# A two-layer encoder trunk: Hyena's transforms modulo 4, their first half moved into the attention, the filter's last layer in high and low parts

## The chip, the cores and the metric

The kernel runs on one core of a Trainium2 chip. The metric is the device time of one execution in microseconds (us), a median over several executions. One further execution is recorded by the hardware profiler. Engines are PE (matrix products; PEld is its loading of stationary operands), DVE and ACT (elementwise work), POOL and SP (here almost only issuers of transfers).

## The reference, cut to what matters

Layer 1 of the trunk has two mixers side by side, a dense attention of eight heads and a Hyena convolution over 512 channels, then a projection with `w_out`. What the change touches is Hyena: a filter made by a small sine network, and a long convolution by Fourier transforms.

```python
def hyena_filter(L, w1, b1, w2, b2, w3, b3, w4, freq):
    ...
    h = (h @ w4.astype(f32)).reshape(L, 2, CONV_WIDTH)
    deltas = jnp.abs(jnp.linspace(HYENA_MIN_DECAY, HYENA_MAX_DECAY, CONV_WIDTH, dtype=f32))
    h = h * jnp.exp(-t[:, :, None] * deltas)
    kfull = jnp.concatenate([h[:, 0], jnp.zeros((1, CONV_WIDTH), f32), h[:0:-1, 1]], axis=0)
    return kfull * lax.rsqrt(jnp.sum(kfull * kfull, axis=0, keepdims=True) + EPS)

def fft_long_conv(u, kfull):
    L = u.shape[1]
    uf = jnp.fft.rfft(u.astype(jnp.float32), n=2 * L, axis=1)
    kf = jnp.fft.rfft(kfull, n=2 * L, axis=0)
    return jnp.fft.irfft(uf * kf[None], n=2 * L, axis=1)[:, :L].astype(u.dtype)

def mixer_cd(...):
    q, k, v = split_qkv(h, qk_g)
    att = blocked_dense_attention(axial_rope(q), axial_rope(k), v)
    u = short_conv(h[..., QKV_COLS:], conv_w, conv_b)
    x0, x1, vh = jnp.split(u, 3, axis=-1)
    kfull = hyena_filter(h.shape[1], f_w1, f_b1, f_w2, f_b2, f_w3, f_b3, f_w4, f_freq)
    z = x1 * vh
    y = x0 * (fft_long_conv(z, kfull) + skip * z)
    return jnp.concatenate([att, y], axis=-1)
```

The sequence is 512 tokens long, the model 1024 wide, everything float32.

## The kernel before, in words

**Layout.** Activations stand channels by tokens, eight tiles of 128 channels by 512 tokens. A dense product in full precision is made of three products of rounded parts: an operand is split into a high part (ACT casts it, line L203) and a low part (DVE subtracts, L204), and PE adds high x high, low x high and high x low. Weights arrive as 128x1024 tiles `raw`, are split into `wh` and `wl`, and are used in `column` (L224 to L226) and `project` (L358, with the residual update on DVE at L363). Small products that are not split are plain float32 matmuls; in the trace each of those is two records.

**Order.** Every engine works through its own queue in order. A scheduler fixes that order when the program is built; pools of tiles add waits. A pool has a fixed number of slots, and a tile that takes a slot waits until the last reader of the slot's former tile is done. The pools that matter here are `x` (8 slots of 128x512), `e3` (2), `wh` and `wl` (5 each), and the banks of the accumulators: A has 3, V 1, Q 2, C 2.

**The filter.** `hyena_filter` (L1011) runs while layer 0's last feed-forward projection is on PE. The last layer multiplies the 64-row `fsrc` by `w4` in 8 plain float32 matmuls of 512 columns (L1029); DVE multiplies by the decay (L1035), sums squares (L1041, L1042), forms sums and differences (L1045) and splits them. Then 96 matmuls of 256 columns (`dft_sums`, through L224 to L226) transform the filter for two halves of the channels and two parts `ft` of the frequencies, `fold` (L970) combines even and odd tokens, and the spectra go to a scratch tensor `spec` (L1073).

**The attention and Hyena.** In `mixer` of layer 1 a loop over j (pairs of heads) issues a query pair, the softmax of heads 2j and 2j+1 (scores L809 and L810 into bank A, row maxima L820 on DVE, exponentials L825 on ACT into `x` tiles, normalisation L834), the attention of the head before (transposes L847, splits into `e3` tiles, products L853 and L854), and `hyena_in(j)`, which needs three dense columns of 24 matmuls each in bank C. After the loop `hyena` runs for both halves: transposes of z (L1093), per half and `ft` a forward transform of 8 float32 matmuls of 256 columns (L1114), a copy on ACT (L974), the fold (L975, L976), products with the filter's spectrum on DVE (L1123, L1124, L1129) whose spectrum tiles arrive through `x` slots (L1105 to L1107), and per tile j an inverse transform of 8 float32 matmuls (L1140), closed by L1144, L1147 and L1150. The projection with `w_out` (`project`, L358) takes the attention's tiles first, so that its matmuls for those stand between Hyena's on PE.

Of the kernel before, what the change touches and what calls it, by code (L numbers as in the profile page):

```python
# [16 lines left out]
F32 = mybir.dt.float32  # L17
# [7 lines left out]
P = 128  # L25
# [99 lines left out]
def constants():  # L125
# [7 lines left out]
    c[:, 132:136] = -t.reshape(2, P, 2).transpose(1, 2, 0).reshape(P, 4)  # L133
# [23 lines left out]
    m = np.arange(256, dtype=np.int64)  # L157
    mats = []
    for fn in (np.cos, np.sin):
        for par in (0, 1):  # L160
            ph = np.outer(2 * m + par, 2 * m + 1) % 2048
            mats.append(fn(ph * (math.pi / 1024)).astype(f))

    def rows(m):
        return m.reshape(2, P, 256).transpose(1, 0, 2).reshape(P, 512)

    dft = np.ascontiguousarray(np.stack(
        [np.concatenate([rows(mats[q]), rows(mats[q + 1])], axis=1) for q in (0, 2)]
        + [np.concatenate([rows(mats[q].T), rows(mats[q + 1].T)], axis=1) for q in (0, 2)]
    ))  # L170
# [17 lines left out]
class Trunk:  # L188
# [26 lines left out]
    def dft_matrix(self, u):  # L215
        hi, lo = self.t("wh", (P, 1024), F32R), self.t("wl", (P, 1024), F32R)
# [676 lines left out]
    def mixer(self, l, key):  # L893
# [22 lines left out]
        for j in range(4):  # L916
# [41 lines left out]
    def dft_sums(self, mats, sp_cos, sp_sin, tags):  # L958

        out = []  # L960
        for par in range(2):
            p = self.ps(tags[par])
            for q, sp in enumerate((sp_cos, sp_sin)):
                for mt in range(2):
                    lhs = [m[:, par * 512 + mt * 256 + self.ft * P :][:, :P] for m in mats[q]]
                    self.mm3(p[:, q * 256 : q * 256 + 256], lhs, sp[par][mt], mt == 0, mt == 1)
            out.append(p)
        return out

    def fold(self, pe, po, plus, minus):  # L970

        nc = self.nc
        o = self.t("th")
        nc.scalar.copy(out=o, in_=po)  # L974
        nc.vector.tensor_add(out=plus, in0=pe, in1=o)  # L975
        nc.vector.tensor_sub(out=minus, in0=pe, in1=o)  # L976
# [34 lines left out]
    def hyena_filter(self):  # L1011

        nc, ap = self.nc, self.ap
        src = self.fsrc
        w4 = self.t("raw", (P, 1024))[:64]
        nc.sync.dma_start(out=w4, in_=ap["f_w4"])
        delta = self.t("rb")
        nc.sync.dma_start(out=delta, in_=ap["delta"])
        asp, bsp = [[], []], [[], []]
# [229 lines left out]
```

## Time and profile before

| | us |
|---|---|
| median of 3 executions | 1874.56 (1872.99 to 1875.28) |
| profiled execution, its time | 1871.36 |
| its span, first to last instruction | 1869.6 |
| PE busy | 1827.3 (98% of the span) |
| DVE busy | 1527.1 (82%) |
| ACT busy | 980.6 (52%) |

The profiled execution is 3.2 us under the median. Its mean granted PE clock is 0.995 of full speed. A busy share is the share of the span in which the engine had an instruction in work; PE's records overlap, so the distance between the starts of two records tells the price of one.

### The profile page before, as it was taken

The page shows a single profiled execution, that of the slowest core. Times are in us where ns is not written, and L with a number is a line of the kernel's source. Part 1 is how long each engine was busy: PE and PEld are TensorE (multiplying, and loading weights), DVE is VectorE, ACT ScalarE, POOL GpSimd, SP SyncE. Part 2 cuts the span into 40 slices and gives each one's busy share as a digit, 9 for nine tenths or more (in the row PEclk, how much of TensorE's full clock was granted, in tenths as well). Part 3 has the DMA queues.
Part 4 walks back from the last instruction along what each step waited for, and adds up shares of the span by engine and source line. Part 5 has one row for each costly group of instructions (what it writes and reads, how often), then busy time and mean ns, then how long its engine had stood idle before and what let it go on. Part 6 is the DMA issues. An engine that isn't in the chain of part 4 may idle for free.

```text
span 1869.6 us, 29686 instructions
## 1 busy us (share of the span) xinstructions
PE 1827.3 (98%) x11628; PEld 1630.7 (87%) x11628; DVE 1527.1 (82%) x2604; ACT 980.6 (52%) x1610; POOL 3.6 (0%) x9
## 2 busy tenths in 40 slices
PE   7999989999999999999999999999999999999999
PEld 5789879888888899799988988979887898898997
DVE  8998879688759889898799996977887879695682
ACT  5435335378837445255563544655788365353460
POOL 0000000000000000000000000000000000000000
PEclk9999989999999999999999999999999999999999
DMA  7863754733232645745326462345222322233231
GB/s 273 280 218 124 263 179 146 237 110 96 91 99 69 201 145 161 275 147 199 127 72 213 163 215 71 103 163 176 80 80 91 125 90 91 91 113 113 91 125 57
DMA packets 83654, 269.22 MB, mean 144 GB/s; under 512 B 10024, under 2 KB 13352, under 8 KB 83514
## 3 DMA queue, kind: packets, MB, share of 16 engines
q1 hardware_dynamic: 81898, 263.13, 42.2%
q0 software_dynamic: 1616, 4.20, 0.6%
q8 instruction: 91, 1.49, 0.3%
q14 instruction: 49, 0.40, 0.1%
HBM read 258.88 MB, written 10.50 MB: 144 GB/s over the span
## 4 chain that ended last, share of the span: by engine, by line
PE 72%; DVE 15%; DMA 9%; ACT 2%; issue 2%; SPq 0%; ACTq 0%; DVEq 0%
PE pA L486 23%; PE pC L358 16%; DVE wl L204 4%; PE pA L358 4%; PE pV L486 4%; DMA raw<-w_mod 3%; DVE raw L248 3%; PE pC L225 2%; PE pC L226 2%; PE pC L224 2%; PE pA L226 2%; DMA raw<-w2b 2%; PE pA L225 2%; PE pA L224 2%; DMA raw<-w 2%
## 5 line engine op out<-in xcount | busy, mean ns | idle before, releaser
L203 ACT CAST wh<-raw 128x1024 fp32r<-128x1024 f32 (+2 forms) x387 | 368.8, 956 | 453.5 <-PE pA L486 134.4
L204 DVE TENSOR_TENSOR wl<-raw,wh 128x1024 fp32r<-128x1024 f32 (+2 forms) x387 | 426.8, 1105 | 78.7 <-ACT wh L203 74.7
L486 PE MATMUL pA<-h,wh 128*128 128x256 f32 x1608 | 297.2, 283 | 8.5 <-DVE tq L518 7.4
L486 PE MATMUL pA<-e,wh 128*128 128x256 f32 x1608 | 295.5, 281 | 5.7 <-ACT tq L517 4.8
L486 PEld LDWEIGHTS pA<-h,wh 128*128 128x128 f32 x1608 | 247.5, 190 | 12.3 <-DVE tq L518 7.8
L486 PEld LDWEIGHTS pA<-e,wh 128*128 128x128 f32 x1608 | 245.8, 189 | 10.8 <-ACT tq L517 8.6
L486 PE MATMUL pA<-h,wl 128*128 128x256 f32 x804 | 226.6, 282 | 0.2 <-DVE wl L204 0.2
L358 PE MATMUL pC<-gb,wh 128*128 128x512 f32 (+1 forms) x800 | 224.8, 367 | 0.0
L486 PE MATMUL pA<-e,wl 128*128 128x256 f32 x804 | 224.4, 279 | 0.0
L248 DVE SCALAR_TENSOR_TENSOR raw<-raw,cond 128x1024 f32<-128x1024 f32 x144 | 175.1, 1220 | 31.1 <-DMA raw<-w_mod 29.7
L358 PE MATMUL pC<-ga,wh 128*128 128x512 f32 (+1 forms) x648 | 186.2, 372 | 7.1 <-DVE x L363 6.6
L358 PEld LDWEIGHTS pC<-gb,wh 128*128 128x128 f32 x800 | 143.6, 188 | 26.9 <-issue 0.8
L486 PEld LDWEIGHTS pA<-h,wl 128*128 128x128 f32 x804 | 151.5, 188 | 0.5 <-DVE wl L204 0.4
L486 PEld LDWEIGHTS pA<-e,wl 128*128 128x128 f32 x804 | 151.3, 188 | 0.0
L358 PEld LDWEIGHTS pC<-ga,wh 128*128 128x128 f32 x648 | 115.2, 189 | 33.6 <-DVE x L363 12.3
L358 PE MATMUL pC<-gb,wl 128*128 128x512 f32 (+1 forms) x392 | 143.4, 366 | 0.0
L363 DVE SCALAR_TENSOR_TENSOR x<-pC,mod,x 128x512 f32<-128x512 f32 (+1 forms) x108 | 73.2, 685 | 83.1 <-PE pC L358 82.6
L226 PE MATMUL pA<-h,wl 128*128 128x256 f32 (+1 forms) x373 | 118.7, 324 | 3.9 <-DVE wl L204 3.9
L225 PE MATMUL pA<-h,wh 128*128 128x256 f32 (+1 forms) x373 | 119.3, 327 | 1.3 <-DVE h L345 1.3
L224 PE MATMUL pA<-h,wh 128*128 128x256 f32 (+1 forms) x373 | 116.0, 323 | 0.0
L358 PE MATMUL pC<-ga,wl 128*128 128x512 f32 (+1 forms) x300 | 110.4, 368 | 0.0
L486 PE MATMUL pV<-h,wh 128*128 128x256 f32 x536 | 99.4, 284 | 0.5 <-DVE tc L557 0.5
(316 smaller groups left out, 3589.2 us busy)
## 6 DMA issues: line engine op xcount, KB each, us to landing
raw<-w SPq DMA_DIRECT2D x164, 512.0 KB, 3.7
raw<-w_mod SPq DMA_DIRECT2D x144, 512.0 KB, 4.2
raw<-w2b SPq DMA_DIRECT2D x64, 512.0 KB, 4.1
raw<-w_in SPq DMA_DIRECT2D x36, 512.0 KB, 4.3
raw<-w2a SPq DMA_DIRECT2D x32, 384.0 KB, 3.7
raw<-w_out SPq DMA_DIRECT2D x16, 512.0 KB, 3.5
raw<-w_start SPq DMA_DIRECT2D x8, 512.0 KB, 5.0
xs<-x SPq DMA_DIRECT2D x16, 256.0 KB, 2.2
```

The source lines that it names most:

```text
L203: self.nc.scalar.copy(out=hi, in_=src)
L204: self.nc.vector.tensor_sub(out=lo, in0=src, in1=hi.bitcast(F32))
L224: mm(out, lhsT=wh, rhs=rh, start=start, stop=False)
L225: mm(out, lhsT=wh, rhs=rl, start=False, stop=False)
L226: mm(out, lhsT=wl, rhs=rh, start=False, stop=stop)
L248: nc.vector.scalar_tensor_tensor(out=raw, in0=raw, scalar=1.0, in1=self.cond, op0=ALU.mult, op1=ALU.mult, accum_out=m[:, c : c + 1])
L358: nc.tensor.matmul(ps, lhsT=lh, rhs=r, start=k == 0 and q == 0, stop=k == n_in - 1 and q == len(todo) - 1)
L363: nc.vector.scalar_tensor_tensor(out=x, in0=ps, scalar=gate[dt], in1=x, op0=ALU.mult, op1=ALU.add)
L486: self.nc.tensor.matmul(out, lhsT=lh, rhs=rr, start=first and n == 0, stop=n == 11, skip_group_check=True)
```

## The change

The transforms split tokens modulo 4 instead of into even and odd ones. Each of the four matrices is 128x512 instead of two tiles of that size; the forward transform of a half is 8 float32 matmuls of 256 columns instead of 16, the inverse transform of a tile j is 8 float32 matmuls of 128 columns instead of 8 of 256, and the filter's transform is 72 split matmuls instead of 96. More is left to DVE: the fold has two stages, and a butterfly stands behind the products. `hyena` takes one half per call. Half 0 is called behind `hyena_in(2)`, inside the attention loop, half 1 where both were called before. Its `h` tiles for half 0 become `gb` tiles, and its matrices live in `gc` and `rb` slots. The filter's last layer multiplies high and low parts: `w4` is loaded twice, into partitions 0 to 63 and 64 to 127, cast and split, and each of the 8 plain matmuls becomes two rounded ones.

```diff
@@ mixer
                 zs.append(self.hyena_in(j, oth[j]))
+                if j == 2:
+                    self.hyena(0, zs, oth, "gb")
...
-        ys = oth if l == 0 else self.hyena(zs, oth)
-        for j, y in enumerate(ys):
+        if l == 1:
+            self.hyena(1, zs, oth, "h")
+        for j, y in enumerate(oth):
             ready(4 + j, y, "h")
@@ fold
+    def fold(self, p, k, swapped=None):
+        nc = self.nc
+        c, d = self.t("tc"), self.t("tc")
+        nc.scalar.copy(out=c, in_=p[2])
+        nc.scalar.copy(out=d, in_=p[3])
+        e, o = self.t("tq"), self.t("tq")
+        nc.vector.tensor_add(out=e, in0=p[0], in1=c)
+        nc.vector.tensor_add(out=o, in0=p[1], in1=d)
+        nc.vector.tensor_add(out=k[0][0], in0=e, in1=o)
+        nc.vector.tensor_sub(out=k[0][1], in0=e, in1=o)
+        e, o = self.t("tq"), self.t("tq")
+        a, b = slice(0, 256), slice(256, 512)
+        nc.vector.tensor_sub(out=e[:, a], in0=p[0][:, a], in1=c[:, a])
+        nc.vector.tensor_sub(out=e[:, b], in0=c[:, b], in1=p[0][:, b])
+        if swapped:
+            p1, p3 = swapped()
+            d = self.t("tc")
+            nc.scalar.copy(out=d, in_=p3)
+            nc.vector.tensor_sub(out=o, in0=p1, in1=d)
+        else:
+            nc.vector.tensor_sub(out=o[:, a], in0=p[1][:, b], in1=d[:, b])
+            nc.vector.tensor_sub(out=o[:, b], in0=p[1][:, a], in1=d[:, a])
+        nc.vector.tensor_add(out=k[1][0], in0=e, in1=o)
+        nc.vector.tensor_sub(out=k[1][1], in0=e, in1=o)
@@ hyena_filter
+        w4 = self.t("raw", (P, 1024))
+        for half in (slice(0, 64), slice(64, 128)):
+            nc.sync.dma_start(out=w4[half], in_=ap["f_w4"])
+        w4h, w4l = self.t("wh", (P, 1024), F32R), self.t("wl", (P, 1024), F32R)
+        nc.scalar.copy(out=w4h, in_=w4)
+        nc.vector.tensor_sub(out=w4l[:64], in0=w4[:64], in1=w4h[:64].bitcast(F32))
+        src = self.t("tc", dtype=F32R)
+        nc.scalar.copy(out=src[:64], in_=self.fsrc)
+        nc.vector.tensor_sub(out=src[64:], in0=self.fsrc, in1=src[:64].bitcast(F32))
...
-                nc.tensor.matmul(p, lhsT=toks, rhs=w4[:, s * T : (s + 1) * T], start=True, stop=True)
+                nc.tensor.matmul(p, lhsT=toks, rhs=w4h[:, s * T : (s + 1) * T], start=True, stop=False)
+                nc.tensor.matmul(p, lhsT=toks[:64], rhs=w4l[:64, s * T : (s + 1) * T], start=False, stop=True)
...
+            p = [self.dft_sums(mats, asum, bsum, s, "QAQA"[s]) for s in range(4)]
+            k = [[self.t("th"), self.t("th")] for _ in range(2)]
+            self.fold(p, k, lambda: [self.dft_sums(mats, asum, bsum, s, t, True) for s, t in ((1, "A"), (3, "V"))])
@@ hyena
+        p = [self.ps(bank) for bank in "CQCQ"]
+        for s in (0, 2, 1, 3):
+            for q in range(2):
+                nc.tensor.matmul(
+                    p[s][:, q * 256 : q * 256 + 256], lhsT=self.fwd[q][:, s * P : (s + 1) * P], rhs=zt[s],
+                    start=True, stop=True)
+        sps = [[self.t("th"), self.t("th")] for _ in range(2)]
+        self.fold(p, sps)
...
+        ys = [None] * 4
+        for par in range(2):
+            u, v = yh[0][par], yh[1][par]
+            w = self.t(tag)
+            if par == 0:
+                a, b = slice(0, 256), slice(256, 512)
+                nc.vector.tensor_add(out=w[:, a], in0=u[:, a], in1=v[:, a])
+                nc.vector.tensor_sub(out=w[:, b], in0=u[:, b], in1=v[:, b])
+                nc.vector.tensor_sub(out=u[:, a], in0=u[:, a], in1=v[:, a])
+                nc.vector.tensor_add(out=u[:, b], in0=u[:, b], in1=v[:, b])
+            else:
+                nc.vector.tensor_add(out=w, in0=u, in1=v)
+                nc.vector.tensor_sub(out=u, in0=u, in1=v)
+            ys[par], ys[par + 2] = w, u
+        for j in js:
             p = self.ps("C")
+            for s in range(4):
+                for q in range(2):
                     o = q * 256 + (j % 2) * P
                     nc.tensor.matmul(
+                        p[:, s * P : (s + 1) * P], lhsT=ys[s][:, o : o + P],
+                        rhs=self.inv[q][:, s * P : (s + 1) * P], start=q == 0, stop=q == 1)
```

How the order moves is seen at three places. In its rows a name ends in the number of the tile; lines are those of the changed kernel, whose scores are L802 and L803, attention transposes L840 and products L846 and L847, columns L217 to L219, forward transform L1119, inverse transform L1168.

On PE before, behind the third column of `hyena_in(2)`, the columns of `hyena_in(3)` (pC_15156, pC_15191) stood between the scores of head 6 (pA):

```order
L809 MATMUL pA_15006<-ga_13955,gb_14648 128x512
L810 MATMUL pA_15006<-ga_13956,gb_14648 128x512
L224 MATMUL pC_15156<-h_13666,wh_15151 128x512
L225 MATMUL pC_15156<-h_13667,wh_15151 128x512
L226 MATMUL pC_15156<-h_13666,wl_15152 128x512
...
L224 MATMUL pC_15191<-h_13654,wh_15186 128x512
...
L809 MATMUL pA_15013<-ga_13955,gb_14648 128x512
```

In the changed kernel the same place on PE holds half 0's transforms (the third column of `hyena_in(2)` is pC_14903, and pC_15282 is the first of `hyena_in(3)`):

```order
L219 MATMUL pC_14903<-h_13686,wl_14899 128x512
...
L803 MATMUL pA_15088<-ga_13974,gb_14663 128x512
L1119 MATMUL pC_14955<-gb_14944,gc_14931 128x256
...
L802 MATMUL pA_15095<-ga_13973,gb_14663 128x512
L803 MATMUL pA_15095<-ga_13974,gb_14663 128x512
L840 MATMUL pA_15108<-cst,x_14751 128x128
...
L846 MATMUL pV_15107<-e_2683_15113,ga_13989 128x512
L1168 MATMUL pC_15047<-rb_14935,gb_15039 128x128
...
L1168 MATMUL pC_15060<-rb_14937,gb_15010 128x128
...
L217 MATMUL pC_15282<-h_13672,wh_15277 128x512
```

No dense column stands any more between the end of pC_14903 and half 0's inverse; the next one stands behind 62 other rows, the inverse among them.

On DVE in the changed kernel, what stands between the taps of that column (L855, L857) and the first inverse matmul's operand gb_15039 (L1155, L1156) is the whole chain of half 0:

```order
L857 SCALAR_TENSOR_TENSOR e_2613_14825<-pC_14903,cols,e_2613_14825 128x511
...
L971 TENSOR_TENSOR tq_14973<-pC_14953,tc_14969 128x512
...
L1138 TENSOR_TENSOR e_2654_14997<-th_14965,x_14987 128x512
...
L1145 TENSOR_TENSOR gb_15007<-e_2654_14997 128x256
...
L1155 TENSOR_TENSOR gb_15039<-gb_15007,gb_15033 128x256
L1156 TENSOR_TENSOR gb_15039<-gb_15007,gb_15033 128x256
...
L813 TENSOR_REDUCE small_15073<-pA_15095 128x1
...
L1161 TENSOR_TENSOR gb_15010<-gb_15010,gb_15036 128x512
```

From L971 to L1161 it is 41 rows, with one row of the attention among them, the last score maximum of head 6 (L813).

On PE at the end of the mixer, before, the first inverse matmuls (L1140) stood behind 22 rows of the projection, and further rows of it between the tiles' inverses. In the changed kernel the forward transform of half 1 is followed by all of the projection's rows on the attention's tiles, 41 of them, and then by the inverse:

```order
L351 MATMUL pA_15567<-gb_15387,wh_15562 128x512
L1119 MATMUL pC_15409<-h_15400,gc_14931 128x256
...
L1119 MATMUL pQ_15412<-h_15407,gc_14933 128x256
L351 MATMUL pA_15567<-gb_15388,wh_15562 128x512
...
L351 MATMUL pV_15672<-gb_15391,wl_15668 128x512
L1168 MATMUL pC_15503<-rb_14935,h_15495 128x128
L1168 MATMUL pC_15503<-rb_14937,h_15495 128x128
```

What moved here is that no row of the projection is left between one tile's inverse and the other's.

## Rows read from the trace of the kernel before

**Rows 1.** The page's first lines: span, then busy time of each engine.
```profile
span 1869.6 us, 29686 instructions
...
PE 1827.3 (98%) x11628; PEld 1630.7 (87%) x11628; DVE 1527.1 (82%) x2604; ACT 980.6 (52%) x1610; POOL 3.6 (0%) x9
```

**Rows 2.** Stretches: length; busy PE, PEld, DVE, ACT, POOL; clock; DMA share, GB/s.
```profile
1232.00:1254.00 22.00, 21.86 (x84) 14.63 (x83) 19.70 (x32) 14.96 (x23) 0.00 (x0) 1.00 0.29 95
...
1300.00:1448.00 148.00, 147.25 (x766) 120.70 (x764) 121.97 (x220) 122.31 (x220) 0.00 (x0) 1.00 0.27 91
1448.00:1488.00 40.00, 39.96 (x186) 34.05 (x184) 36.81 (x73) 10.81 (x18) 0.00 (x0) 1.00 0.45 145
```

**Rows 3.** Timeline of PE, filter: start, duration, line, tiles, count.
```profile
1228.39 1.99 PE L1029 MATMUL pQ<-raw,rb 64*128 64x512 f32 x4
1230.31 0.73 PE L358 MATMUL pC<-ga,wh 128*128 128x512 f32 x2
...
1258.93 0.28 PE L224 MATMUL pQ<-e,wh 128*128 128x256 f32 x1
...
1259.99 0.40 PE L358 MATMUL pC<-ga,wh 128*128 128x512 f32 x1
```

**Rows 4.** Timeline of PE, transposes, Hyena and the projection around it.
```profile
1394.68 0.87 PE L1093 MATMUL pQ<-cst,e 128*128 128x128 f32 x6
1395.31 0.48 PE L224 MATMUL pC<-h,wh 128*128 128x512 f32 x1
...
1454.35 1.03 PE L1114 MATMUL pC<-h,tq 128*128 128x256 f32 x4
1455.22 1.03 PE L1114 MATMUL pQ<-h,gc 128*128 128x256 f32 x4
...
1465.30 0.39 PE L358 MATMUL pA<-gb,wl 128*128 128x512 f32 x1
1465.53 0.62 PE L358 MATMUL pA<-gb,wh 128*128 128x512 f32 x2
...
1481.23 7.07 PE L1140 MATMUL pC<-ga,h 128*128 128x256 f32 x32
1487.95 0.81 PE L358 MATMUL pA<-h,wh 128*128 128x512 f32 x2
```

**Rows 5.** Timeline of DVE: attention's taps, splits and maxima, then Hyena's products.
```profile
1420.12 0.75 DVE L862 SCALAR_TENSOR_TENSOR e<-pC,cols,e 128x511 f32<-128x511 f32 x1
...
1430.10 1.23 DVE L204 TENSOR_TENSOR wl<-raw,wh 128x1024 fp32r<-128x1024 f32 x1
1431.24 0.69 DVE L204 TENSOR_TENSOR e<-pA,e 128x512 fp32r<-128x512 f32 x1
1431.84 1.28 DVE L820 TENSOR_REDUCE small<-pA 128x1 f32<-128x512 f32 x2
...
1462.40 1.28 DVE L1123 TENSOR_TENSOR e<-th,x 128x512 f32<-128x512 f32 x2
1463.60 0.75 DVE L1124 TENSOR_TENSOR e<-e 128x256 f32<-128x256 f32 x2
...
1466.15 1.42 DVE L1129 TENSOR_TENSOR h<-e 128x256 f32<-128x256 f32 x4
1467.49 0.68 DVE L975 TENSOR_TENSOR th<-pC,th 128x512 f32<-128x512 f32 x1
```

**Rows 6.** Timeline of ACT, the copy of a transform.
```profile
1457.14 0.59 ACT L974 COPY th<-pQ 128x512 f32<-128x512 f32 x1 [2.35 <-PE pQ L1114]
```

**Rows 7.** Timeline of PE, an earlier stage's longest wait, in brackets with its releaser.
```profile
265.10 0.80 PE L486 MATMUL pA<-h,wh 128*128 128x256 f32 x2 [6.77 <-DVE tq L518]
...
270.39 0.60 PE L486 MATMUL pA<-e,wh 128*128 128x256 f32 x2
```

**Rows 8.** Stretches behind that wait, columns as in the earlier group.
```profile
267.00:269.00 2.00, 2.00 (x11) 2.00 (x11) 0.70 (x1) 1.05 (x1) 0.00 (x0) 0.50 0.85 334
...
271.00:273.00 2.00, 2.00 (x19) 2.00 (x19) 1.80 (x4) 1.42 (x3) 0.00 (x0) 1.00 0.55 217
```

More of the change, by code (lines that the diff above doesn't have):

```diff
@@ L132, in constants @@
     t = np.linspace(0.0, 1.0, T, dtype=f)
-    c[:, 132:136] = -t.reshape(2, P, 2).transpose(1, 2, 0).reshape(P, 4)
+    c[:, 132:136] = -t.reshape(P, 4)
     a["cst"] = c
@@ L215, in dft_matrix @@
     def dft_matrix(self, u):
-        hi, lo = self.t("wh", (P, 1024), F32R), self.t("wl", (P, 1024), F32R)
+        hi, lo = self.t("wh", (P, 1024), F32R)[:, :T], self.t("wl", (P, 1024), F32R)[:, :T]
         self.nc.gpsimd.dma_start(out=hi, in_=self.ap["dft_hi"][u])
@@ L1066, in hyena_filter @@
         for half in range(2):
-            cut = lambda sp: [[[v[:, half * 256 : half * 256 + 256] for v in pair] for pair in par] for par in sp]
-            for self.ft in range(2):
-                pe, po = self.dft_sums(mats, cut(asp), cut(bsp), "QQ")
-                k = [self.t("th"), self.t("th")]
-                self.fold(pe, po, *k)
+            cut = lambda sp: [[v[:, half * 256 : half * 256 + 256] for v in pair] for pair in sp]
+            asum, bsum = cut(asp), cut(bsp)
+            p = [self.dft_sums(mats, asum, bsum, s, "QAQA"[s]) for s in range(4)]
@@ new lines, in hyena @@
+        if half == 0:
+            mats = []
+            for u, home in enumerate(("gc", "gc", "rb", "rb")):
+                m = self.t(home)
+                nc.sync.dma_start(out=m, in_=self.ap["dft"][u])
+                mats.append(m)
+            self.fwd, self.inv = mats[:2], mats[2:]
+        js = (2 * half, 2 * half + 1)
+        zt = [None] * 4
+        for par in range(2):
+            p = self.ps("Q")
+            for n in range(2):
+                for j in range(2):
+                    toks = zs[js[j]].rearrange("p (r s) -> p s r", s=4)[:, par + 2 * n]
+                    o = n * 256 + j * P
+                    nc.tensor.transpose(p[:, o : o + P], toks, self.ident)
+            z = self.t(tag)
+            nc.scalar.copy(out=z, in_=p)
+            zt[par], zt[par + 2] = z[:, :256], z[:, 256:]
@@ new lines, in hyena @@
+        p = [self.ps(bank) for bank in "CQCQ"]
[6 more added lines that the diff above has]
+        self.fold(p, sps)
+        yh = []
+        for ft, sp in enumerate(sps):
+            ks = []
+            for s in range(2):
+                k1, k2 = self.t("x"), self.t("x")
+                src = self.spec[half, ft, s]
+                nc.sync.dma_start(out=k1, in_=src)
+                nc.sync.dma_start(out=k2[:, :256], in_=src[:, 256:])
+                nc.sync.dma_start(out=k2[:, 256:], in_=src[:, :256])
+                ks.append((k1, k2))
+            ms = [[v[:, :T], v[:, T:]] for v in (self.t("e3", (P, 1024)), self.t("e3", (P, 1024)))]
+            for s in range(2):
+                for q, op in enumerate((ALU.subtract, ALU.add)):
+                    m = ms[q][s]
+                    nc.vector.tensor_mul(out=m, in0=sp[s], in1=ks[s][q])
+                    nc.vector.tensor_tensor(out=m[:, :256], in0=m[:, :256], in1=m[:, 256:], op=op)
+            pair = []
+            for par, op in enumerate((ALU.add, ALU.subtract)):
+                y = self.t(tag)
+                for q in range(2):
+                    o = (1 - q if (ft, par) == (1, 1) else q) * 256
+                    nc.vector.tensor_tensor(
+                        out=y[:, o : o + 256], in0=ms[q][0][:, :256], in1=ms[q][1][:, :256], op=op)
+                pair.append(y)
+            yh.append(pair)
@@ new lines, in hyena @@
+        ys = [None] * 4
+        for par in range(2):
+            u, v = yh[0][par], yh[1][par]
[10 more added lines that the diff above has]
+            ys[par], ys[par + 2] = w, u
```

123 lines of the change are left out of this document (21 added, 102 removed).

## The prediction

> **What bounds the kernel now.** I read the page first: PE is busy for 1827.3 of 1869.6 us, DVE for 82% of the span, ACT for 52% [rows 1]. A busy PE is not yet a bound, since its records overlap, so I went to the three stretches that the change touches. Around the filter, from 1232 to 1254, PE is busy for 21.86 of 22 us, but DVE for 19.70 as well; in layer 1's attention, from 1300 to 1448, PE has work for 147.25 of 148 us; in Hyena and the projection around it, from 1448 to 1488, for 39.96 of 40, DVE for 36.81 [rows 2]. The timelines then show PE's records there at a steady pitch without brackets. So PE is the bound in all three, by a queue that always holds other work while DVE finishes a transform. What the change takes from PE is gained in full as long as that cover stays; what PE then waits for is lost in full, for it has no slack to catch up with.
>
> **What it removes from PE.** Prices are distances from start to start.
> - Filter's last layer: two plain matmuls take 1.92 us (1228.39 to 1230.31) [rows 3], so 8 take 7.7. A rounded matmul of 512 columns takes 0.23 (1465.30 to 1465.53) [rows 4]; 16 take 3.7. Saved 4.0.
> - Filter's transform: 9 matmuls between 1258.93 and 1259.99 give 0.118 each [rows 3]; 24 fewer save 2.8.
> - Forward transform: four records, two matmuls, in 0.87 [rows 4], 0.435 each; 16 fewer save 7.0.
> - Inverse transform: 32 records, 16 matmuls, in 6.72 [rows 4], 0.42 each, 13.4 for 32. With 128 columns the trace has no plain product; the nearest row is the transpose, six records in 0.63, 0.105 a record [rows 4]. Two records make 0.21, and 32 take 6.7. That is the lower end; if little fixed cost hides in it, 0.25 is the upper (some 60% of the row with 256 columns). I take 0.21, since halving 0.42 gives the same. Saved 6.7, at the other end 5.4.
>
> The Trainium skill (TensorE: Matmul & The Clock Gate, section Back-to-back issue gap) gives about 81 ns for a matmul of 128 columns with its weight load in a stream; by it the inverse would take 5.2 us and the time would be 1.5 us lower. The transposes' 0.105 is measured on this kernel's float32 data, so it decides.
>
> Together PE loses 20.5 us of work. The transposes stay 16; the dense columns and the projection keep theirs. Halved transform matrices and fewer loads are worth nothing: the loads have no wait on PE in these stretches.
>
> **What it adds on DVE.** An operation on 128x512 has a pitch of 0.60 (L1123's pair takes 1.20, 1462.40 to 1463.60), one on 128x256 of 0.335 (L1129's four, 1466.15 to 1467.49), and the split of a weight takes 1.14 [rows 5]. A half was two blocks of 6 operations of 0.60 and 8 of 0.335, 12.6 us. In the changed kernel a half costs: fold 6x0.60 + 4x0.335 = 4.94, products 8x0.60 + 16x0.335 = 10.16, butterfly 2x0.60 + 4x0.335 = 2.54, 17.6 in all. The 5 us more would not matter if they were covered. But before, a product could begin behind the first quarter of a half's forward transform, and the inverse of half 0 ran while half 1 was multiplied; now each half is one chain: copy, fold, products, butterfly, inverse.
>
> **Half 0 in the attention.** Time 0 is the end of PE's third column for pair 2 (pC_14903). By the order, PE then passes two transposes, forward products and scores of head 6. The last forward group (pC_14955) takes the bank of that column, free when DVE has done both taps; ahead of them and among them in DVE's queue are four splits of attention tiles (2.4), a weight's split (1.1), two further sums and products (1.2), two maxima (1.3), small rows (some 0.6), and the taps themselves (1.4), 8.0 [rows 5]; with some 0.6 of it done by time 0 the release is at 7.4 and the forward's end, one group of 0.87 later, at about 8.25. ACT's first copy (0.59 [rows 6]) lets DVE begin at 9.0. To the first inverse operand there are the fold, the products and two of the butterfly's rows, 15.8 us: 24.8. The 16 inverse matmuls need 3.4, with a wait for the last butterfly row, and end at 28.7; one attention product and the release of a bank follow, and the next column starts at 30.8. The work that PE has in between: forward 3.5, inverse 3.4, scores and attention products some 20 at 0.233, transposes some 18 at 0.105, 13.4 in all. Most of that is late, too: head 6's exponentials want `x` slots that hold spectra until DVE's products are done (about 20), its last score wants an accumulator that those exponentials free, and the attention's splits want the two `e3` slots that the products use. So PE idles 30.8 - 13.4 = 17.4 us, and I add 1 for the softmax of head 6, which is late afterwards. The bounds: with DVE at the taps at once (ACT's pass of about 0.6 and 1.4 for both) the whole chain starts 5.4 earlier, 12 us are left, and 10.5 without any lag; with the second spectra's loads, which wait for the first products' slots, 3 us late, it is 21.5.
>
> **Half 1 at the end.** Time 0 is the last column's end. Transposes, seven projection matmuls and the forward end at 5.9. Then 41 projection matmuls, 9.5 us, last until 15.4. DVE begins at 6.1 and again needs 15.8: the inverse starts at 21.9. PE idles 6.5, and 0.7 within the inverse: 7.2 us, between 4 (DVE starts early) and 9.
>
> **Filter.** `w4` takes a `wh` and a `wl` slot that the projection's weights had, and DVE, already at 19.70 of 22 us, gets two more splits, 1.75 us; ACT gets two casts. I expect two waits on PE of about 1.8 us for a weight's split, 3.5 together, between 0 and the 6.8 that were saved there.
>
> **Clock.** After PE had waited 6.77 us, 24 matmuls of 256 columns took 5.29 us (265.10 to 270.39) [rows 7], 0.22 each against 0.118, so 2.5 us more, at a granted clock of 0.50 [rows 8], the lower of its two levels, 1.2 GHz. The wait for half 1's chain is about as long, that for half 0's longer, with short work in it. I add 2.5 for half 0, whose inverse comes right behind the wait, and 2.0 for half 1: 4.5, between 0 and 9.
>
> **Sum.** -20.5 + 3.5 + 18.4 + 7.2 + 4.5 = +13.1. On the profiled execution's 1871.36 that is 1884.5; the median of the runs is 3.2 higher, so 1887.7, and I say 1887: slower by 0.7%.
>
> **Rivals.** About 0.2% (3.7 us) is what a measurement of this kernel can tell from no change.
> - A, the cover holds (faster). PE's wait at half 0 shrinks to 2 us with no loss of clock there. For it speaks that before, DVE's four blocks, 25 us, lay wholly behind PE's work [rows 2]; against it that PE meets no dense column until the inverse is done. The sum is then -20.5 + 3.5 + 2 + 7.2 + 2.0 = -5.8, a median of 1868.8. The other terms leave 7.8 of the saving, so the case is faster by over 3.7 where this wait is under 4.1.
> - B, about the same. DVE has no backlog when pair 2 ends, so 12 us idle at half 0, and the filter's saving stays: -20.5 + 1 + 12 + 5 + 2.5 = 0: 1874.6.
> - C, the clock stays at half through both places. PE gets only short pieces between waits there. Then half 0's path has the forward's end, the inverse and two attention pieces doubled, about 7 in place of 2.5; half 1's 41 matmuls take 19 instead of 9.5 and end at 25, 3 behind DVE's chain, and its inverse doubles, so 6.4 in place of 2.0: 9 more, 1896.6. Against it: 6 us behind the long wait, with dense work, the clock was 1.00 again [rows 8].
>
> The Trainium skill (TensorE: Matmul & The Clock Gate, section A second HAM failure mode: psum-queue depth-cycling) tells of a kernel whose short pauses between groups of matmuls made the clock go to and fro between its levels; by that rule C is the likelier one. No row here shows short pauses doing it.
>
> **Chances.** My sum with its smaller errors (1878.3 to 1893): 0.59; A 0.10; B 0.15, of which a few hundredths fall on either side of no change; C 0.16. So faster 0.12, same 0.13, slower 0.75. The range leaves out the low part of A and the worst of C: 1869 to 1897; the likeliest case's own is 1880 to 1893.
>
> **What would show it.** Right: on PE, one wait of some 10 us or more before the first L1168 after the third pair, released by DVE, with the clock at half behind it; a wait of 6 to 7 before L1168 at the end of the mixer; L1168 at 0.21 and L1119 at 0.435; waits of 1 to 2 for `wl` near the filter. Wrong: dense columns that run while DVE works on half 0, taps done 2 us after the column's end, no half clock, or an inverse that costs as much as before.

## The result, and the profile after

The changed kernel takes 1893.3 us (median of 4 executions, 1885.3 to 1894.2), the kernel before 1873.8 beside it: the ratio is 1.010, 95% interval 1.0081 to 1.0119. It is slower by 1%; the forecast was 1887.

The profiled execution is the one of 1885.3 us, the fastest of the four; the others took 1892.8 to 1894.2. What follows explains the profiled one. Its page begins:

```profile
span 1883.5 us, 29619 instructions
...
PE 1816.4 (96%) x11572; PEld 1622.6 (86%) x11572; DVE 1543.5 (82%) x2640; ACT 986.0 (52%) x1616; POOL 3.6 (0%) x9
```

Against [rows 1], PE has 10.9 us less to do and the span is 13.9 longer, so PE stands idle some 25 us more. The view of PE's waits, from the filter to the mixer's end (line, what it waited for, us in total, times, longest), says where; before, this stretch had one wait of 0.6.

```profile
PE pA L802 <- ACT x L818: 7.3, 1, 7.3
PE pC L1168 <- DVE h L1155: 6.3, 1, 6.3
PE pQ L1112 <- DVE tq L986: 2.9, 1, 2.9
PE pC L1119 <- DVE e L857: 1.8, 1, 1.8
PE pC L351 <- DVE wl L197: 1.8, 1, 1.8
PE pC L351 <- ACT e L196: 1.3, 1, 1.3
PE pQ L1112 <- ACT tc L969: 1.2, 1, 1.2
PE pV L846 <- ACT e L196: 1.0, 1, 1.0
PE pA L218 <- DVE h L338: 0.6, 1, 0.6
PE pC L351 <- DVE x L356: 0.5, 1, 0.5
PE pQ L1119 <- ACT gb L1114: 0.5, 1, 0.5
PE pC L1168 <- DVE gb L1160: 0.2, 1, 0.2
```

The first two L351 waits (1.8 and 1.3) are the filter's, the third (0.5) stands later in the same projection. L1168 by h is half 1, and L218 is the wait that the kernel before has as well. The other seven are half 0, 14.8 us together. PE's timeline there (its column ends at 1415.17) shows one long halt in pieces:

```profile
1423.30 1.64 PE L1119 MATMUL pC<-gb,gc 128*128 128x256 f32 x4 [1.85 <-DVE e L857]
1426.11 0.49 PE L1112 MATMUL pQ<-cst,e 128*128 128x128 f32 x1 [1.16 <-ACT tc L969]
1429.47 0.49 PE L1112 MATMUL pQ<-cst,e 128*128 128x128 f32 x1 [2.87 <-DVE tq L986]
1437.27 0.79 PE L802 MATMUL pA<-ga,gb 128*128 128x512 f32 x1 [7.31 <-ACT x L818]
...
1441.21 0.50 PE L846 MATMUL pV<-e,ga 128*128 128x512 f32 x1 [0.95 <-ACT e L196]
1441.55 1.05 PE L1168 MATMUL pC<-rb,gb 128*128 128x128 f32 x8
1442.80 2.94 PE L1168 MATMUL pC<-rb,gb 128*128 128x128 f32 x24 [0.19 <-DVE gb L1160]
1445.50 0.48 PE L847 MATMUL pV<-e,ga 128*128 128x512 f32 x1
...
1447.70 0.39 PE L217 MATMUL pC<-h,wh 128*128 128x512 f32 x1
```

Each piece names another releaser. The first three (0.46, 1.85 and 1.16, 3.5 us together) end with ACT's copy of a transpose, with DVE's taps and with ACT's copy of the forward transform, ahead of the chain or at its start. Behind the 2.87, the 7.31 and the 0.19 stands the same run of DVE's queue, which in DVE's timeline works without a gap from 1425.60 (L971) to 1443.9 (L1161); the 0.95 is head 6's attention, late after them. At the end of the mixer it is simpler, the projection's last row and then nothing until the butterfly is done:

```profile
1490.02 0.40 PE L351 MATMUL pV<-gb,wl 128*128 128x512 f32 x1
1496.67 6.46 PE L1168 MATMUL pC<-rb,h 128*128 128x128 f32 x32 [6.25 <-DVE h L1155]
1502.88 0.71 PE L351 MATMUL pA<-h,wh 128*128 128x512 f32 x2
```

The clock by stretch (the column ahead of the last two; columns as in [rows 2]) is at the lower level through the halt at half 0, back at the upper one for its inverse, and low again for the whole inverse of half 1:

```profile
1422.00:1424.00 2.00, 0.70 (x3) 0.62 (x4) 1.96 (x5) 0.00 (x0) 0.00 (x0) 0.93 0.32 129
1430.00:1432.00 2.00, 0.00 (x0) 0.00 (x0) 2.00 (x5) 0.00 (x0) 0.00 (x0) 0.50 0.35 115
1438.00:1440.00 2.00, 2.00 (x10) 1.55 (x8) 2.00 (x6) 0.87 (x2) 0.00 (x0) 0.50 0.00 0
1442.00:1444.00 2.00, 1.81 (x16) 1.61 (x15) 2.00 (x6) 0.17 (x1) 0.00 (x0) 1.00 0.03 8
...
1498.00:1500.00 2.00, 2.00 (x11) 2.00 (x10) 1.94 (x4) 0.00 (x0) 0.00 (x0) 0.50 0.03 8
```

**A ruler for the experiments.** The stages ahead of the filter are the same in all kernels, yet a profile reaches `w4`'s first product anywhere from 1222.6 to 1228.9 us. So I compare stretches within each profile, cut at four matmuls in PE's timeline: `w4`'s first; the first of 256 columns in the feed-forward's last projection (cut A; 1271.26 before); the one of the mixer's first columns that waits about 0.6 for a normalised tile (cut B; 1300.77 before); the first of 256 columns in the projection behind the mixer (end). Expectations speak of filter and mixer by cut A, in the last experiment by cut B. In the last two kernels the first matmul of 256 columns comes some 12 us earlier, so that cut A is left out for them. In us:

| kernel | filter to A | A to end | filter to B | B to end | ratio to before (95%) |
|---|---|---|---|---|---|
| before | 46.95 | 229.13 | 76.46 | 199.62 | |
| changed | 47.76 | 243.76 | 78.05 | 213.47 | 1.0100 (1.0081 to 1.0119) |
| changed again | 48.19 | 244.47 | 78.51 | 214.15 | 1.0083 (1.0065 to 1.0101) |
| both halves at the end | 49.06 | 241.64 | 79.38 | 211.32 | 1.0079 (1.0062 to 1.0096) |
| half 0's inverse late | 48.75 | 235.11 | 79.07 | 204.79 | 1.0040 (1.0025 to 1.0055) |
| spectra in raw | 47.84 | 251.65 | 78.16 | 221.33 | 1.0129 (1.0113 to 1.0144) |
| low matmul, 128 rows | 45.08 | 244.56 | 75.41 | 214.23 | 1.0081 (1.0061 to 1.0101) |
| results split early | 47.69 | 237.60 | 78.00 | 207.29 | 1.0052 (1.0036 to 1.0067) |
| filter's last layer alone | 49.58 | 229.13 | 79.05 | 199.66 | 1.0014 (1.0004 to 1.0024) |
| inverse at head 7 | 45.67 | 237.77 | 75.97 | 207.47 | 1.0045 (1.0032 to 1.0057) |
| inverse after the forward | 45.42 | 237.60 | 75.72 | 207.30 | 1.0026 (1.0017 to 1.0035) |
| spread | 45.51 | 230.56 | 75.83 | 200.24 | 0.9995 (0.9985 to 1.0005) |
| spread, other slots | - | - | 74.68 | 207.94 | 1.0026 (1.0016 to 1.0037) |
| spread, behind head 6 | - | - | 73.64 | 202.77 | 1.0003 (0.9993 to 1.0014) |

The changed kernel loses 1.6 us in the filter and 13.9 in the mixer by cut B, 15.4 in all; its profile's span is 13.9 longer because it came to the filter 1.7 earlier.

### The profile page after: what moved, and what is told of

It is laid out like the page before. It is cut to its first block, busy times and chain, and to the rows that moved or that the text cites. A ratio compares the mean times of both kernels' runs of the same rounds, so it can differ in the third digit from the quotient of the medians.

```text
span 1883.5 us, 29619 instructions
## 1 busy us (share of the span) xinstructions
PE 1816.4 (96%) x11572; PEld 1622.6 (86%) x11572; DVE 1543.5 (82%) x2640; ACT 986.0 (52%) x1616; POOL 3.6 (0%) x9
## 3 DMA queue, kind: packets, MB, share of 16 engines
q0 software_dynamic: 1616, 3.15, 0.5%
## 4 chain that ended last, share of the span: by engine, by line
PE 68%; DVE 18%; DMA 9%; ACT 2%; issue 2%; SPq 0%; ACTq 0%; DVEq 0%
PE pA L479 21%; PE pC L351 17%; DVE wl L197 5%; DMA raw<-w_mod 4%; PE pA L351 4%; PE pV L479 3%; DVE raw L241 3%; PE pC L218 2%; PE pC L219 2%; PE pC L217 2%; PE pA L219 2%; PE pA L218 2%; PE pA L217 2%; DMA raw<-w 2%; DMA raw<-w2b 1%
## 5 line engine op out<-in xcount | busy, mean ns | idle before, releaser
L351 PE MATMUL pC<-gb,wh 128*128 128x512 f32 (+1 forms) x800 | 225.8, 368 | 0.0
L351 PE MATMUL pC<-ga,wh 128*128 128x512 f32 (+1 forms) x648 | 186.9, 374 | 10.8 <-DVE x L356 9.4
L351 PEld LDWEIGHTS pC<-gb,wh 128*128 128x128 f32 x800 | 144.6, 189 | 27.0 <-DVE gb L552 0.4
L351 PEld LDWEIGHTS pC<-ga,wh 128*128 128x128 f32 x648 | 115.6, 190 | 36.2 <-DVE x L356 13.8
L351 PE MATMUL pC<-gb,wl 128*128 128x512 f32 (+1 forms) x392 | 143.9, 367 | 0.0
L356 DVE SCALAR_TENSOR_TENSOR x<-pC,mod,x 128x512 f32<-128x512 f32 (+1 forms) x108 | 73.2, 685 | 84.3 <-PE pC L351 83.9
L219 PE MATMUL pA<-h,wl 128*128 128x256 f32 (+1 forms) x373 | 118.2, 322 | 3.9 <-DVE wl L197 3.9
L218 PE MATMUL pA<-h,wh 128*128 128x256 f32 (+1 forms) x373 | 118.5, 325 | 1.3 <-DVE h L338 1.3
L217 PE MATMUL pA<-h,wh 128*128 128x256 f32 (+1 forms) x373 | 115.4, 322 | 0.0
L351 PE MATMUL pC<-ga,wl 128*128 128x512 f32 (+1 forms) x300 | 111.9, 373 | 1.8 <-DVE wl L197 1.8
```

The costliest lines, as they stand in the source:

```text
L217: mm(out, lhsT=wh, rhs=rh, start=start, stop=False)
L218: mm(out, lhsT=wh, rhs=rl, start=False, stop=False)
L219: mm(out, lhsT=wl, rhs=rh, start=False, stop=stop)
L351: nc.tensor.matmul(ps, lhsT=lh, rhs=r, start=k == 0 and q == 0, stop=k == n_in - 1 and q == len(todo) - 1)
L356: nc.vector.scalar_tensor_tensor(out=x, in0=ps, scalar=gate[dt], in1=x, op0=ALU.mult, op1=ALU.add)
```

## The experiments

**Both halves at the end.**
```diff
-                if j == 2:
-                    self.hyena(0, zs, oth, "gb")
...
+            self.hyena(0, zs, oth, "h")
             self.hyena(1, zs, oth, "h")
```


> The changed kernel with both halves called behind the attention loop (half 0's tiles from the h slots). Theory, the chain: a half now needs about 16 us of DVE work between its forward and its inverse, and only one half's chain finds cover, the 47 projection matmuls (11 us); PE waits about 5 us before the first inverse and about 16 before the second, 20 to 21 together against 21 in the changed kernel, so the time is within 5 us of it, 1880 to 1895. Rival, the place: what costs is that half 0 stands in the attention; then the attention's 14.8 us of waits go, nothing comes in their place, and the kernel is faster than before, 1860 to 1870.

Measured: 1887.6 us, and two waits ahead of the inverses (timeline of PE):
```profile
1473.21 5.29 PE L1167 MATMUL pC<-rb,h 128*128 128x128 f32 x32 [4.99 <-issue]
...
1497.76 2.47 PE L1167 MATMUL pC<-rb,h 128*128 128x128 f32 x10 [15.79 <-DVE h L1154]
```
5.0 and 15.8, as the theory said. For the first the view names no releaser (`issue`); DVE's first butterfly row there, L1154, ends 0.1 us ahead of it. The place is not what costs: the chain needs cover wherever it stands, and two chains need it twice.

**Half 0's inverse late.** Its last part becomes a function of its own.
```diff
-                    self.hyena(0, zs, oth, "gb")
+                    ys0 = self.hyena(0, zs, oth, "gb")
...
+        if l == 1:
+            self.hyena_back(0, ys0, zs, oth)
         mix = {}
```


> The changed kernel with half 0's forward, fold, products and butterfly behind the third pair as they are, and its inverse behind the attention loop; by the order 48 dense matmuls then follow the forward directly. Theory, the queue: PE waited because the dense columns of pair 3 stood behind the inverse; the waits between the third pair and those columns fall from 14.8 us to under 5, some 5 come back behind the loop, where head 7 has no dense work left beside it, and the time falls by 6 to 12 us against the changed kernel. Rival, the slots: head 6 waits for x and e3 slots in any case, the waits only move behind the columns, 12 us or more of them, and the time falls by under 3.

Measured: A to end 8.7 us shorter. 3.0 us of waits lie ahead of the columns, 3.4 behind them, against 14.8:
```profile
1425.54 1.10 PE L1121 MATMUL pC<-gb,gc 128*128 128x256 f32 x4 [1.85 <-DVE e L857]
...
1427.31 0.79 PE L217 MATMUL pC<-h,wh 128*128 128x512 f32 x1 [0.68 <-ACT tc L970]
...
1441.80 0.50 PE L802 MATMUL pA<-ga,gb 128*128 128x512 f32 x1 [1.44 <-ACT x L818]
```
So most of the halt was the queue: dense work that could have run stood behind an inverse that could not.

**Spectra in raw slots.**
```diff
-                k1, k2 = self.t("x"), self.t("x")
+                kk = self.t("raw", (P, 1024))
+                k1, k2 = kk[:, :T], kk[:, T:]
```


> The changed kernel with the filter's spectra in slots of the raw weights instead of the x slots that head 6's exponentials want. Theory, the queue: the wait for an exponential (7.3 us) goes, but the same time is then spent before the inverse, which needs DVE's chain; the waits at half 0 stay within 3 us of 14.8. Rival, the slots: head 6's exponentials run on time, so do the scores and the attention products behind them, and the waits fall by 6 us or more.

Measured: head 6's scores no longer wait, and the time is spent ahead of the inverse:
```profile
1443.53 6.23 PE L1169 MATMUL pC<-rb,gb 128*128 128x128 f32 x32 [11.27 <-issue]
```
The view names no releaser for the 11.27; DVE's first butterfly row, L1156, ends 0.1 us ahead of that inverse. The waits at half 0 are 14.3 in place of 14.8. The `x` slots were a releaser and not the cause. The kernel is slower still, for half 1's spectra now hold back the projection's weights (11.4 us for a cast of `wh` at the end), which I had not foreseen.

**Low matmul over 128 rows.** It adds the product of the two low parts.
```diff
-        nc.vector.tensor_sub(out=w4l[:64], in0=w4[:64], in1=w4h[:64].bitcast(F32))
+        nc.vector.tensor_sub(out=w4l, in0=w4, in1=w4h.bitcast(F32))
...
-lhsT=toks[:64], rhs=w4l[:64, s * T : (s + 1) * T]
+lhsT=toks, rhs=w4l[:, s * T : (s + 1) * T]
```


> The changed kernel with the filter's low matmul (L1047) over all 128 rows instead of 64; it then adds the product of the two low parts as well. Theory: a pair of high and low took 0.88 us on PE instead of the 0.466 that I had reckoned since PE changes between 128 and 64 rows; with 128 rows in both the low one falls from 0.55 to 0.33 or less, 1.7 us over 8. Rival: the stationary operand is read with a stride of 4 elements, its load takes 0.305 instead of 0.19, and both stay as they are (0.33 and 0.55).

Timeline of PE, the changed kernel and then this one:
```profile
1236.46 0.40 PE L1046 MATMUL pQ<-wh,tc 128*128 128x512 f32 x1
1236.79 0.61 PE L1047 MATMUL pQ<-wl,tc 64*128 64x512 f32 x1
1237.34 0.50 PE L351 MATMUL pC<-ga,wh 128*128 128x512 f32 x1
```
```profile
1234.22 0.40 PE L1046 MATMUL pQ<-wh,tc 128*128 128x512 f32 x1
1234.46 0.39 PE L1047 MATMUL pQ<-wl,tc 128*128 128x512 f32 x1
1234.69 0.39 PE L351 MATMUL pC<-ga,wl 128*128 128x512 f32 x1
```
A pair falls from 0.88 us to 0.47, the price of the prediction; that is 3.3 over 8 pairs, of which 0.5 is lost to longer waits in the filter, and the filter gets 2.7 shorter, more than the 1.7 expected. The loads of the stationary operand still take 0.31, so the stride is not the cause by itself. But it sets the size. In the kernel with the filter's last layer alone (below), where the stride is 2, the low matmul (L1036) takes 0.43:
```profile
1235.69 0.40 PE L1035 MATMUL pQ<-wh,tc 128*128 128x512 f32 x1
1236.01 0.50 PE L1036 MATMUL pQ<-wl,tc 64*128 64x512 f32 x1
1236.44 0.50 PE L358 MATMUL pC<-ga,wh 128*128 128x512 f32 x1
```
The loads of the low matmul, in the changed kernel and then in that one (by form: total us, mean ns, idle before):
```profile
L1047 PEld LDWEIGHTS pQ<-wl,tc 64*128 64x128 f32 x8 | 2.4, 305 | 1.9 <-issue 1.7
```
```profile
L1036 PEld LDWEIGHTS pQ<-wl,tc 64*128 64x128 f32 x8 | 1.5, 190 | 2.2 <-issue 2.0
```
Over the 0.23 of the low matmul with 128 rows these are 0.32 more with a load of 0.305, and 0.20 more with one of 0.19: the 64-row matmul pays about the time of its own load, which is covered when all have 128 rows. That the change of the row count does it, and not the 64 rows, the kernel before shows. There a run of two 64-row records takes 1.07 us, and one of four 1.92 [rows 3]:
```profile
1231.20 1.13 PE L1029 MATMUL pQ<-raw,rb 64*128 64x512 f32 x2
1232.27 0.73 PE L358 MATMUL pC<-ga,wh 128*128 128x512 f32 x2
```
So two further records take 0.85, 0.43 each, twice the 0.2175 of the forward's records with half the columns and 128 rows; within a run the 64 rows cost nothing extra. Theory and rival each have a part.

**The splits of half 0's results early.**
```diff
+        if l == 1:
+            for j in range(2):
+                ready(4 + j, oth[j], "h")
         if l == 1:
             self.hyena(1, zs, oth, "h")
```


> The changed kernel with one thing moved: the splits of half 0's two results stand ahead of half 1's transforms, so that by the order 65 instead of 41 projection matmuls lie between half 1's forward and its inverse. Theory, the cover: 24 more at 0.233 are 5.6 us; the wait before the last inverse falls from 6.25 to about 1 us, the clock stays at the upper level there and the inverse takes 3.5 instead of 6.2; 8 us less in all against the changed kernel, whose profile is 1885 and whose median 1893. Rival, DVE: the two results' splits (4 operations) and what else moves ahead on DVE delay the chain as much as PE gains, and the time falls by under 3.

Measured: median 1884.2, A to end 6.2 us shorter. The wait falls to 0.7, a later one of 0.4 joins it, and the inverse runs at the upper clock:
```profile
1503.07 1.13 PE L1171 MATMUL pC<-rb,h 128*128 128x128 f32 x8 [0.70 <-DVE h L1158]
1504.59 2.94 PE L1171 MATMUL pC<-rb,h 128*128 128x128 f32 x24 [0.39 <-DVE h L1163]
1508.48 0.97 PE L351 MATMUL pA<-h,wh 128*128 128x512 f32 x3 [0.95 <-ACT h L196]
```
A new wait of 0.95 for the last results' casts takes back a part, since nothing else is left for PE there; so 6 rather than 8.

**The filter's last layer alone.** In the kernel before, the change's lines for `w4`, `w4h`, `w4l` and `src`, and
```diff
-lhsT=toks, rhs=w4[:, s * T : (s + 1) * T], start=True, stop=True)
+lhsT=toks, rhs=w4h[:, s * T : (s + 1) * T], start=True, stop=False)
+lhsT=toks[:64], rhs=w4l[:64, s * T : (s + 1) * T], start=False, stop=True)
```


> The kernel before with the filter's last layer alone in high and low parts. Theory, slots and splits: PE gains only 0.6 us on the products, and waits of about 3 us for a weight's cast and split come in with a stretch of half clock, 1 us, as in the changed kernel, so it is 2 to 4 us slower than before. Rival, the fold: those waits came from the second stage of the filter's fold on DVE and from the transforms modulo 4, and then this kernel is the same as before or 1 us faster.

Measured: 2.6 us longer to cut A, the mixer the same to 0.05. The waits are 2.3 and 0.2 for casts of `wh` and 0.6 for a split, 3.1 together like the changed kernel's, and there is no second stage of the fold here; so the fold is not needed for them. They are put down to other rows than in the changed kernel, where 1.3 ends with ACT's cast of an `e` tile, so that they are the same waits is not shown. The pair takes 0.75 here, so PE gains some 1.7 on the products and not 0.6.

**Three edits, the inverse at head 7**: low matmul over 128 rows, early splits, and
```diff
                 now = self.softmax(l, hd, qs[j])
+                if l == 1 and hd == 7:
+                    self.hyena_back(0, ys0, zs, oth)
```


> Three edits to the changed kernel: half 0's inverse behind the last head's scores instead of directly behind its products; the low matmul over all 128 rows; the splits of half 0's results ahead of half 1's transforms. Theory: the waits at half 0 fall from 14.8 to about 5 us, the one at the end from 6.25 to about 1, PE's half clock behind it goes, the low matmuls save 2 us; from 1883.5 us of span to 1862 to 1868, so faster than before (1869.6) by 0.1 to 0.4%. Rival, the softmax: heads 6 and 7 are late behind DVE's chain and the three waits come back as waits for attention tiles, 1870 to 1876.

A miss: A to end 237.8. All 16 inverse matmuls still came ahead of pair 3's first column (1442.11 to 1449.63 in PE's timeline), since the code of those comes later. The same five waits stand in the trace, 7.3 among them. The gain is the other two edits'.

**The inverse behind half 1's forward.**
```diff
+            ys1 = self.hyena(1, zs, oth, "h")
+            self.hyena_back(0, ys0, zs, oth)
             for j in range(2):
                 ready(4 + j, oth[j], "h")
```


> As the kernel before it in this list, but half 0's inverse stands behind half 1's forward, so that it covers a part of half 1's chain; by the order 16 inverse matmuls and 47 projection matmuls, 14.5 us, lie between them and half 1's inverse, and attention matmuls among the forward. Theory: a wait of 1 to 3 us at the end, about 5 in the attention, a span of 1862 to 1868. Rival: half 0's closing operations on DVE (L1147 and L1150 before) stand in half 1's chain and lengthen it by 2.5 us; the wait at the end is over 4, and the span above 1868.

The rival held: half 1's inverse needs a bank that half 0's closing operation on DVE (L1185) frees, and that stands behind half 1's butterfly:
```profile
1490.92 6.75 PE L1178 MATMUL pC<-rb,h 128*128 128x128 f32 x32 [5.98 <-DVE th L1185]
```

**Spread.** The early splits and 128 rows again, the inverse between the second and third column of pair 3, and
```diff
+    def hyena_in(self, j, x0, between=None):
...
+        if between:
+            between()
...
-        p = [self.ps(bank) for bank in "CQCQ"]
+        p = [self.ps(bank) for bank in ("CQAQ" if half == 0 else "CQCQ")]
```


> Half 0's parts spread: its third forward group goes to a score bank instead of the column's, its inverse stands behind the first two columns of pair 3, the splits of its results ahead of half 1's transforms, and the filter's low matmul takes 128 rows. By the order 48 dense matmuls follow the forward directly, and 70 projection matmuls, 16.3 us, lie between half 1's forward and its inverse. Theory, cover: a chain of 16 us on DVE costs PE nothing where it has that much work in its queue; waits of 14.8 + 6.25 fall to 5 or less, the mixer takes 220 to 226 us instead of 243.8 (before: 229.1) and the filter 45 (before: 47.0), so 1863 to 1870, faster than before by 0.2 to 0.5%. Rival, DVE and ACT: the attention has no room for 18 us in one piece on DVE, heads 6 and 7 are late whatever PE's order is, waits of 10 us or more for attention tiles remain, and the mixer takes 229 or more, no faster than before.

Measured: 1872.8, the same as before, A to end 230.6. At the end 0.75 us are left, at half 0
```profile
1422.45 0.47 PE L217 MATMUL pC<-h,wh 128*128 128x512 f32 x1 [2.00 <-DVE e L857]
...
1439.84 0.50 PE L802 MATMUL pA<-ga,gb 128*128 128x512 f32 x1 [4.30 <-ACT x L818]
```
Both sides were half right: the waits at the two places fell from 21.1 to 9.0 (0.58 more at head 6, 0.39 and 0.95 more at the end), but the mixer did not come below that of before. The 4.30 stands behind DVE again, where head 6's first maximum ends at 1438.2, behind the butterfly. The granted clock was 0.50 behind both waits shown (1424 to 1426 and 1442 to 1446), which by double prices costs some 4 us more (an estimate from these rows). Waits and clock together use up the 13.2 us that the transforms save in the mixer.

**The changed kernel again.**


> The changed kernel once more, unchanged. Its profiled execution was 1885.3 us and three others 1892.8 to 1894.2. If the 8 us are chance in the stages ahead of the change, which have waits of their own, the new executions scatter between 1884 and 1895, and the mixer in the new profile again takes 243 to 245. If it is the changed places that are bistable (a longer stretch at half clock), most are at 1893 and a profiled one of that kind shows a mixer of 250.

1885.4, 1889.4 (profiled), 1890.3 and 1893.9; A to end 244.5, the filter 48.2. The two profiles agree on the changed places within 1.2 us, though 4 apart in time. No execution at 1893 was profiled. Its mean granted clock is 0.986, against 0.988 and 0.989 in the profiled ones, so it had more time at the lower level, and where is not shown. That it lies ahead of the change is likely: `w4`'s start is spread over 6 us, the kernel before scatters as widely (1869.3 to 1878.6 in 79 executions), and the eight executions of the changed kernel lie 16.8 above it on average (1890.6 against 1873.9), close to the 15.4 and 16.6 that the two profiles lose between the filter and the end.

**Spread, other slots.** Half 0's spectra and `w4h`, `w4l` in `raw` slots.
```diff
-        w4h, w4l = self.t("wh", (P, 1024), F32R), self.t("wl", (P, 1024), F32R)
+        w4h, w4l = self.t("raw", (P, 1024), F32R), self.t("raw", (P, 1024), F32R)
...
+                if half == 0:
+                    kk = self.t("raw", (P, 1024))
+                    k1, k2 = kk[:, :T], kk[:, T:]
```


> The kernel of the run before, with two slot changes: half 0's spectra in slots of the raw weights (half 1's stay in x), and the filter's last layer in raw slots instead of one wh and one wl slot. The order now sets 48 columns between head 6's and head 7's attention matmuls. Theory, slots: head 6's exponentials run while DVE multiplies, the wait of 4.3 for them and the half clock behind it go, and the mixer takes 221 to 227 us instead of 230.6; the projection's weights keep their slots, the two waits in the filter (2.3 and 1.8) go and it takes 40 to 42 instead of 45.5; together 1858 to 1866, faster than before by 0.4 to 0.8%. Rival, DVE: maxima and splits of heads 6 and 7 stand behind DVE's chain whatever slots there are, so waits of 4 us or more come back at attention transposes, and the raw slots taken delay weights; mixer 229 or more, filter 45 or more.

The filter's two waits went (to B 74.7), as the theory said, but one of 3.8 came just behind (x, L356). In the mixer the rival held: waits of 6.9 and 1.4 for columns whose weights found no `raw` slot, and 4.0 for head 6 in spite of its free `x` slots, behind the chain on DVE:
```profile
1433.61 0.79 PE L217 MATMUL pC<-h,wh 128*128 128x512 f32 x1 [6.92 <-ACT wh L196]
...
1441.45 0.79 PE L802 MATMUL pA<-ga,gb 128*128 128x512 f32 x1 [4.02 <-ACT x L818]
```

**Spread, behind head 6**, with `w4h` and `w4l` in `raw`.
```diff
                 pending = now
+                if l == 1 and hd == 6:
+                    ys0 = self.hyena(0, zs, oth, "gb")
```


> The spread kernel (half 0's inverse behind the first two columns of pair 3, its results' splits early, a score bank for one forward group, the low matmul over 128 rows, spectra in x) with half 0's transforms behind head 6's scores instead of ahead of them, and the filter's last layer in raw slots. By the order some 15 dense matmuls stand among the forward and 39 behind it before the last head's scores are all through. Theory, DVE's queue: head 6's maxima now stand ahead of the chain, its exponentials and attention run beside it, so the wait of 4.3 us for them and the half clock behind it go, or come back smaller at head 7; the mixer's stretch (to the projection's second part) takes 195 to 199 us against 200.2 in the spread kernel and 199.6 before, the filter's 74.7 against 76.5 before; 2 to 6 us faster than before. Rival: the chain in one piece only puts the wait on head 7, the mixer stays at 200 or more, and the kernel is the same as before, within 2 us.

The rival held. Head 6 runs through, and head 7 pays for all of it:
```profile
1447.91 0.80 PE L802 MATMUL pA<-ga,gb 128*128 128x512 f32 x1 [10.24 <-ACT x L818]
```
No version beat the kernel before; spread and this one equal it.

## Why the prediction was right, step by step

- **Mechanism.** Right: PE got most of the saving, and lost more where a half's chain on DVE had no cover. The inverse of half 1 began 21.75 us after the last column (reckoned 21.9), the column behind half 0's came at 32.5 (30.8). One sign did not come: the halt at half 0 is no single wait before L1168. It is in seven pieces, the longest (7.3) before a score, and L1168 then starts without a wait and at the upper clock.
- **What PE saves.** Predicted 20.5; by the prices measured it is 16.7. The forward (0.86 for two matmuls, 7.0) and the filter's transform held. The inverse at full clock takes 2.70 for 12 matmuls (1442.80 to 1445.50), 0.225 each, 6.2 saved for 6.7. The step that was mis-sized is the filter's last layer: I priced both matmuls at 0.23, from a run of 128-row matmuls, and a pair takes 0.88, so 0.7 was saved for 4.0. The low matmul over 128 rows shows the cause, the change of the row count.
- **Half 0.** 14.8 us of waits for 17.4, and the 1 of late softmax is in it. PE had a little more to do meanwhile at half clock. The late inverse takes 8.4 of the 14.8 away and the spectra in raw next to nothing, so most of it is the queue and not the slots. The time of the taps came out by luck: they ended 8.0 us after the column (reckoned 7.4), but some 2 us of the list on DVE were done by time 0, and for 2.0 DVE stood idle, above all for head 6's first score, until 1416.93.
- **Half 1.** 6.25 for 7.2, shown by the early splits.
- **Filter.** 3.1 for 3.5, where I had two waits for a split. One is (1.8). The other, 1.3, is put down to ACT's cast of an `e` tile, and DVE's L356, which frees a bank of C, ends some 0.1 us ahead of that cast; which of the two PE waited for is open. That the slots cause these waits is shown only so far: in raw slots they go, and a wait of 3.8 comes behind them.
- **Clock.** Predicted 4.5, measured 6.4. Half 1's inverse took 6.21 in place of 3.6, 2.6 more (2.0 reckoned). For half 0 I had put 2.5 on the inverse, which ran at the upper clock; scores, transposes and the forward's end at double price cost some 2.3 in its place, so the size was luck. The filter's 1.5, 7 matmuls in 3.15 us from 1249.86, I had not counted.
- **Sum.** -16.7 + 3.1 + 14.8 + 6.25 + 6.4 = 13.9, against 15.4 in the stretch. Of the 1.5 left, 0.55 is the third L351 wait (1276.75, for DVE's L356), and 1 is not accounted for. What PE saves was 3.8 too high and the clock 1.9 too low, the waits 4.9 too high: the errors cancel, and that my +13.1 came so near is luck. From the profiled execution to the median I added 3.2, as in the kernel before; it was 8.0. That is most of the 6 us between forecast and result, and its place is open (the changed kernel again).
- **Rivals.** A needed cover at half 0, and PE met no dense column there before 1447.70. B needed the taps early; they came at 8.0, less by a backlog than by the order, which put head 6's maxima ahead of them. Of C a part came: the forward's end and the attention's pieces at half 0 ran at half clock, but its inverse and half 1's 41 matmuls did not. The clock fell once at each place. At half 0 it was back behind 3.0 us of scores and transposes (1437.27 to 1440.25), at half 1 it stayed at 0.50 from 1496 to 1502, over 5 us of inverse without a pause. The Trainium skill (TensorE: Matmul & The Clock Gate, A second HAM failure mode: psum-queue depth-cycling) made C the likelier; this trace shows no to and fro, though half 0's short pieces stayed low for 17 us (1424 to 1441).

## What to carry to other kernels

Less work for the engine that bounds a kernel pays only while the queue in front of it stays full: count, for every chain handed to another engine, how much independent work lies behind its start in the bounding engine's own order, and price the difference with the clock's fall. Where the trace names a slot or a bank, test it by moving the slot: here the `x` slots, once free, handed the same wait to the next releaser, until independent work was put in its place. Before splitting one long chain over two places, look at what the other queue (here the softmax's maxima on DVE) has to wait for behind it.

## What the hardware showed unexpectedly

A matmul of 64 rows and 512 columns between matmuls of 128 rows costs 0.55 us, the same one over 128 rows 0.23. A stationary operand read with a stride of 4 elements loads in 0.31 instead of 0.19 (stride 2: 0.19). Among matmuls of 512 columns and one row count that costs nothing, but where the row count changes the load's time is paid: 0.55 with the load of 0.305, 0.43 with that of 0.19.

The Trainium skill (TensorE: Matmul & The Clock Gate, Why this matters for your kernels) gives a single matmul over 32 rows the same time as one over 128. Within a run of 64-row matmuls this case agrees (0.43 for a plain record, twice the 0.2175 of one with 128 rows and half the columns); for a single one between matmuls of 128 rows it does not hold here.
